# A DiT block kernel: the first residual's gate is summed in the merge loop instead of in the linear-attention heads

## The chip, the cores and the metric

The kernel runs on one core of a Trainium2 chip. The metric is the device time of one execution in microseconds; the lower the better. TensorE does the matmuls, VectorE, ScalarE and GpSimd the elementwise work, and SyncE issues the large DMAs.

## What is computed

One layer of a diffusion backbone on 512 latent tokens of width 1024, with 256 context tokens. A conditioning vector `c` gives, through one large matrix, six rows of 1024: shift, scale and gate of the token half, and shift, scale and gate of the channel half.

```python
mod = jax.nn.silu(c) @ w_ada[layer] + b_ada[layer]
sh1, sc1, gt1, sh2, sc2, gt2 = jnp.split(mod[:, None, :], 6, axis=-1)
h = modulate(rms_norm(x_lat, norm1_g[layer]), sh1, sc1)
mix, mix_c = token_mixer(h, hc, ...)      # MLA branch, GLA branch, sigmoid-gated merge, @ w_out
x_lat = x_lat + gt1 * mix
h = modulate(rms_norm(x_lat, norm2_g[layer]), sh2, sc2)
x_lat = x_lat + gt2 * conv_ffn(h, ...)
return rms_norm(x_lat, final_g)
```

`gt1` is the gate of the first residual. It is needed only when the merged branches have been multiplied by `w_out`. `sh2` and `sc2` are needed a little later, when the normalised rows are modulated for the channel half.

## The kernel before

Almost every matmul is done three times (`mm3`, L125 to L128) on operands split into a high and a low part. A split (`split`, L119 to L122) is a ScalarE cast for the high part and a subtraction, on GpSimd for most weights, for the low one. So a weight tile goes from a raw tile (three in turn, tag `raw`), filled by a DMA of the SyncE queue, through ScalarE and GpSimd into `whi` and `wlo` (four in turn each), and only then to TensorE.

The stages follow one another: the projections, eight heads of attention, the values of the linear attention (`gla_v`), four linear-attention heads, the merge loop over eight column blocks j of 128, `w_out` with the first residual and the second norm, the up projection with the convolution, and the down projection.

The modulation rows of the second half are made in parts of 256 columns by `mod_part` (L217). A part loads two tiles of 512 KB of `w_ada` and runs eight VectorE instructions over 128x256 elements (L227 once, L229 seven times), which leave in `mp` a sum over eight blocks of rows; the 128 partitions are still to be summed. `mod_fin` (L242) does that for shift and scale parts by two small matmuls with a column of ones (`mod_small`, L232) and a VectorE addition into `modsh2` or `modsc2`. `mod_bcast` (L255) does it for a gate part by a matmul of `ones` broadcast to 128x128 with the 256 columns, and adds the result into the gate's tile. Twelve parts are made ahead of `w_out`: eight of shift and scale (0 to 7) and four of the gate `gt1`.

In the kernel before, parts 0 and 1 are summed during the last attention heads and parts 2 and 3 during `gla_v`. Every linear-attention head h sums gate part h and, in its second half, part 4 + h; the last of each kind falls into the merge loop.

A linear-attention head does, on TensorE and in this order: transposes of the decayed keys (`to_tokens`, L875: those of the context from `C1` at L881, those of the latent tokens from `T1` at L885), the chunk states (`states`, L890) and the products within a chunk (`output`, L909). Before the states can start, VectorE has to copy the context transposes out of PSUM into `C2` (L882), and ScalarE those of the latent tokens into `T1` (L886, L887). The same VectorE also does the keys' and queries' scaling of the head (`apply`, L853), four passes over 128x1024 elements. In PSUM there are four single-bank tiles (`pb`) and two of two banks (`p2`, shown as `p` in the views).

The instruction order on each engine is set by a scheduler that simulates the program (`schedule_with_timeline_sim`), within the data dependences and the order in which tiles are handed out; the engines then run these lists strictly in order.

Of the kernel before, what the change touches and what calls it, by code (L numbers as in the profile page):

```python
# [9 lines left out]
F32 = mybir.dt.float32  # L10
# [62 lines left out]
def block_kernel(ctx: ExitStack, tc: tile.TileContext, p, out):  # L73
# [51 lines left out]
    def mm3(o, sh, sl, mh, ml, first, last):  # L125
        PE.matmul(o, lhsT=sh, rhs=mh, start=first, stop=False)  # L126
        PE.matmul(o, lhsT=sh, rhs=ml, start=False, stop=False)  # L127
        PE.matmul(o, lhsT=sl, rhs=mh, start=False, stop=last)  # L128

# [50 lines left out]
    def view(name):  # L180
# [4 lines left out]
                                         view("w_down"))  # L185

    def load_cols(w, c0, n=128, k0=0, k1=KT):
        r = raw_tile()
        SY.dma_start(out=k3(r, k1 - k0, n), in_=w[:, k0:k1, c0:c0 + n])
        return r  # L190
# [60 lines left out]

    def mod_norm2(j, tile_):
        return mod_part(3072 + j * 256, mp_tile(), tile_)

    def mod_bcast(acc, dst):  # L255

        ps = pb()
        mm(ps[:, 0:256], ones.broadcast_to([128, 128]), acc)
        tt(V, dst, dst, ps[:, 0:256], ALU.add)


# [28 lines left out]
    with tc.tile_pool(name="e1", bufs=1) as e1:  # L290
# [462 lines left out]
        for h in range(NH):  # L753
            P = softmax(h, q2s[h])
            if h == 0:
                for t in range(2, 6):
                    values(t)
                q2s.append(prep_q(1))
            if h + 1 < NH:
                prep_k(h + 1)  # L760
            if h + 2 < NH:
                q2s.append(prep_q(h + 2))
            if h == 5:
                gla_v_weights(0)
            attend(h, P)
            if h == 6:
                parts = [mod_norm2(0, S4f)]
            elif h == 7:
                parts.append(mod_norm2(1, S4f))
        heads_out(*pend[0])  # L770
        gla_v_weights(1)
        for t in range(6):
            gla_v(1, t)
            if t in (1, 3):
                mod_fin(t // 2, parts[t // 2])
                parts.append(mod_norm2(t // 2 + 2, S4f))

    def sigmoid(dst, ps):
        A.activation(dst, ps, AF.Exp, scale=-1.0)
        A.activation(dst, dst, AF.Ln, bias=1.0)  # L780
        A.activation(dst, dst, AF.Exp, scale=-1.0)

# [6 lines left out]
    with tc.tile_pool(name="egl", bufs=1) as eg:  # L789
# [192 lines left out]
        gr = gate(0)  # L982
        mod_fin(2, parts[2])
        mod_fin(3, parts[3])
        to_tokens(dec)
        for h in range(GH):
            St = states(h, dec)
            on = output(h, dec, Q, St)
            part = mod_part(2048 + h * 256, mp_tile(), S4f)
            if h + 1 < GH:  # L990
                dec = decay(h + 1)
                merge_mla(2 * h)
                kq = proj_kq(h + 1)
            else:
                merge_mla(2 * h)
                merge_mla(2 * h + 1)
            gate_out(h, on, gr)
            if h + 1 < GH:
                Q = apply(kq, dec)
                gr = gate(h + 1)  # L1000
                to_tokens(dec)
                mod_bcast(part, gt1[:, h * 256:(h + 1) * 256])
                part = mod_norm2(4 + h, S4f)
                merge_mla(2 * h + 1)
                mod_fin(4 + h, part)

# [7 lines left out]

    def load_wo(k):
        r = raw_tile()
        SY.dma_start(out=r, in_=w_out[:, k, :])
        h_, l_ = S4([128, 1024]), S4([128, 1024])
        split(h_, l_, r, V if k in (5, 7) else G)
        wo.append((h_, l_))  # L1020
# [11 lines left out]
    with tc.tile_pool(name="emg", bufs=1) as em_:  # L1032
        def merge_weights(j):
            return (split_w(load_cols(w_in, CGB + j * 128)), split_w(load_cols(w_brg, j * 128, k1=4), 512))

        ahead = merge_weights(0)
        for j in range(8):
            wgb, wbg = ahead
            gb = pb()
            proj(wgb, gb)  # L1040
            if j + 1 < 8:
                ahead = merge_weights(j + 1)
            bg = pb()
            for k in range(4):
                mm3(bg, k3(wbg[0], 4, 128)[:, k, :], k3(wbg[1], 4, 128)[:, k, :], yT[k][:, 0, :], yT[k][:, 1, :], k == 0,
                    k == 3)
            sg = tl(em_, [128, 512], F32, "sg", 2)
            sigmoid(sg, gb)
            tt(V, sg, bg, sg, ALU.mult)
            tt(V, sg, sg, m1[j // 2][:, j % 2, :], ALU.add)  # L1050
            mg[j] = S4([128, 2, 512])
            split(mg[j][:, 0, :], mg[j][:, 1, :], sg, V)
            if j in (1, 2, 3, 5):
                load_wo(len(wo))
            if j == 0:
                mod_bcast(part, gt1[:, 768:1024])
                part = mod_norm2(7, lambda: tl(em_, [128, 1024], F32, "xn", 2))
            elif j == 2:
                mod_fin(7, part)
        for k in range(4, 8):  # L1060
# [3 lines left out]
        def w_out_norm(t):  # L1064
            cs = slice(t * 128, (t + 1) * 128)
            mp = p2()
            for k in range(8):
                for half in range(2):
                    hs = slice(half * 512, (half + 1) * 512)
                    mm3(mp[:, hs], mg[k][:, 0, cs], mg[k][:, 1, cs], wo[k][0][:, hs], wo[k][1][:, hs], k == 0, k == 7)  # L1070
            xn = tl(em_, [128, 1024], F32, "xn", 2)
            for half in range(2):
# [202 lines left out]
```

## Time and profile before

| what | us |
|---|---|
| three runs: median | 931.99 |
| lowest and highest | 930.17, 933.8 |
| the profiled execution: its own time | 931.91 |
| its span, first to last instruction | 930.1 |
| TensorE busy in the span | 893.0 |

The profiled execution's time is 1.8 us more than its span, which is what lies around the program, and stands at the median of the runs. Times in the views count from the span's start. The linear-attention heads run from about 236 to 442 us, the merge loop from about 443 to 509 us.

### The profile page before, as it was taken

Reading aid. Unit: us, or ns where it says so; the run is one execution under the profiler, and the core shown is the slowest. Engines: PE = TensorE matmul, PEld = TensorE weight load, DVE = VectorE, ACT = ScalarE, POOL = GpSimd, SP = SyncE. Lnnn points to the kernel's source line nnn. Section 1 sums busy time; section 2 is a strip of 40 time slices with the busy share of each in tenths; the row PEclk is TensorE's granted clock in tenths of the full one; section 3 lists DMA queues with packets and bytes.
Section 4 is the critical chain, followed back from the end, with each engine's and each line's share of the span. In section 5 each row is a group of like instructions: output and inputs, shape, how many; then the busy total and the mean of one; then the engine's idle time right before and its main releaser. Section 6 shows DMA issues by size and latency. Waiting matters only on the chain. (4 is left out here: it accounts for less than half of the span.)

```text
span 930.1 us, 13004 instructions
## 1 busy us (share of the span) xinstructions
PE 893.0 (96%) x5012; PEld 760.0 (82%) x5012; DVE 599.8 (64%) x986; ACT 395.1 (42%) x653; POOL 383.7 (41%) x226
## 2 busy tenths in 40 slices
PE   4989999999989999999999999999999999999995
PEld 3768788899978888888888889888888888888884
DVE  3569987867886998984534484988687876300007
ACT  3445566764534545452445332443424333323102
POOL 3355133563232425242464621344445344466415
PEclk9999999999999999999999999999999999999998
DMA  9863000043341525152644521534343432244002
GB/s 302 258 168 103 1 1 1 9 129 110 107 125 35 161 66 162 55 158 69 212 139 125 164 63 47 157 92 146 103 137 90 136 109 96 73 158 154 23 1 90
DMA packets 131230, 100.77 MB, mean 108 GB/s; under 512 B 5755, under 2 KB 122723, under 8 KB 131169
## 3 DMA queue, kind: packets, MB, share of 16 engines
q1 hardware_dynamic: 130240, 97.83, 34.9%
q0 software_dynamic: 816, 2.09, 0.7%
q8 instruction: 39, 0.64, 0.3%
q14 instruction: 23, 0.18, 0.1%
q10 hardware_dynamic: 112, 0.04, 0.0%
HBM read 97.65 MB, written 2.10 MB: 107 GB/s over the span
## 5 line engine op out<-in xcount | busy, mean ns | idle before, releaser
L118 POOL TENSOR_TENSOR wlo<-raw,whi 128x1024 fp32r<-128x1024 f32 (+2 forms) x113 | 259.0, 2299 | 325.8 <-ACT whi L122 302.6
L126 PE MATMUL pb<-s,whi 128*128 128x512 f32 (+1 forms) x625 | 242.7, 388 | 0.1
L128 PE MATMUL pb<-s,wlo 128*128 128x512 f32 (+1 forms) x625 | 240.5, 385 | 0.0
L127 PE MATMUL pb<-s,whi 128*128 128x512 f32 (+1 forms) x625 | 240.2, 384 | 0.0
L122 ACT CAST whi<-raw 128x1024 fp32r<-128x1024 f32 (+1 forms) x108 | 106.2, 985 | 177.6 <-issue 76.6
L128 PEld LDWEIGHTS pb<-s,wlo 128*128 128x128 f32 x625 | 117.6, 188 | 23.1
L127 PEld LDWEIGHTS pb<-s,whi 128*128 128x128 f32 x625 | 117.7, 188 | 22.9 <-issue 0.7
L126 PEld LDWEIGHTS pb<-s,whi 128*128 128x128 f32 x625 | 117.7, 188 | 22.8 <-DVE modsc L115 0.3
L1146 DVE SCALAR_TENSOR_TENSOR ac<-pb,cwT,ac 128x441 f32<-128x441 f32 (+2 forms) x160 | 110.9, 693 | 19.1 <-ACT ac L1137 15.2
L115 DVE TENSOR_TENSOR ot<-p,gt 128x512 f32<-128x512 f32 x4 | 2.6, 686 | 98.2 <-PE p L128 98.2
L126 PE MATMUL pb<-whi,s 128*128 128x256 f32 (+1 forms) x168 | 55.2, 330 | 0.0
L229 DVE SCALAR_TENSOR_TENSOR mp<-s,csilu,mp 128x256 f32<-128x256 f32 x77 | 54.2, 715 | 1.5
L127 PE MATMUL pb<-wlo,s 128*128 128x256 f32 (+1 forms) x168 | 55.1, 328 | 0.0
L128 PE MATMUL pb<-whi,s 128*128 128x256 f32 (+1 forms) x168 | 55.0, 328 | 0.0
L126 PE MATMUL p<-s,s 128*128 128x512 f32 (+1 forms) x130 | 48.0, 370 | 5.3 <-DVE s L404 3.6
L686 POOL TENSOR_SCALAR P<-P,rs 128x768 f32<-128x768 f32 x32 | 29.4, 924 | 52.0 <-DVE rs L685 51.0
L127 PE MATMUL p<-s,s 128*128 128x512 f32 (+1 forms) x130 | 47.3, 365 | 0.3 <-DVE s L118 0.3
L128 PE MATMUL p<-s,s 128*128 128x512 f32 (+1 forms) x130 | 47.2, 363 | 0.0
L118 POOL TENSOR_TENSOR s<-raw,s 128x1024 fp32r<-128x1024 f32 (+1 forms) x14 | 33.3, 2389 | 26.7 <-ACT s L122 26.7
L128 PE MATMUL p<-s,wlo 128*128 128x256 f32 (+1 forms) x130 | 43.1, 331 | 0.0
L126 PE MATMUL p<-s,whi 128*128 128x256 f32 (+1 forms) x130 | 43.0, 331 | 0.0
L127 PE MATMUL p<-s,whi 128*128 128x256 f32 (+1 forms) x130 | 42.8, 329 | 0.0
(278 smaller groups left out, 1736.2 us busy)
## 6 DMA issues: line engine op xcount, KB each, us to landing
raw<-in_w_up_dram SPq DMA_DIRECT2D x44, 512.0 KB, 3.8
raw<-in_w_in_dram SPq DMA_DIRECT2D x32, 512.0 KB, 3.8
s<-in_w_ada_dram SPq DMA_DIRECT2D x30, 512.0 KB, 6.3
raw<-in_w_down_dram SPq DMA_DIRECT2D x22, 512.0 KB, 3.3
raw<-in_w_ada_dram SPq DMA_DIRECT2D x16, 512.0 KB, 4.8
raw<-in_w_out_dram SPq DMA_DIRECT2D x8, 512.0 KB, 3.4
kT<-in_w_in_dram SPq DMA_DIRECT2D x8, 320.0 KB, 5.3
s<-in_x_dram SPq DMA_DIRECT2D x4, 512.0 KB, 6.3
```

Source lines behind the costliest of these rows:

```text
L115: return eng.tensor_tensor(out=out_, in0=a, in1=b, op=op)
L118: eng.tensor_tensor(out=out_, in0=a, in1=b, op=ALU.subtract)
L122: A.copy(hi, src)
L126: PE.matmul(o, lhsT=sh, rhs=mh, start=first, stop=False)
L127: PE.matmul(o, lhsT=sh, rhs=ml, start=False, stop=False)
L128: PE.matmul(o, lhsT=sl, rhs=mh, start=False, stop=last)
L229: V.scalar_tensor_tensor(out=acc, in0=r3[:, k, :], scalar=c_, in1=acc, op0=ALU.mult, op1=ALU.add)
L686: G.tensor_scalar(out=pt, in0=pt, scalar1=rs, scalar2=1.0, op0=ALU.mult, op1=ALU.mult)
L1146: V.scalar_tensor_tensor(out=a3[:, r0:r1, c0:c1], in0=g3[:, r0 + dy:r1 + dy, c0 + dx:c1 + dx], scalar=cw(dy, dx), in1=a3[:, r0:r1, c0:c1], ...
```

## The change

The gate parts leave the heads. In the merge loop, blocks j = 0 to 3 each sum one gate part, straight into a quarter of one two-bank PSUM tile (`gsum`), from `w_ada` tiles of the pool `xn`, which gets three buffers instead of two; block 4 sums part 7 of the scale, in PSUM too. In block 6 ScalarE copies both sums to SBUF, and after block 7's matmuls two matmuls of 512 columns take the place of the four of 256 columns (`mod_bcast`), with two additions into `gt1`. The first four `w_out` tiles also load into `xn` instead of `raw`.

Parts 3 to 6 of the second norm are now begun in heads 0 to 3, one each, and the two small matmuls that end a part come one head later, behind `merge_mla` of the next head; those of parts 2 and 3 thus no longer stand ahead of the first head.

```diff
@@ attention heads and gla_v
-            if h == 6:
-                parts = [mod_norm2(0, S4f)]
-            elif h == 7:
-                parts.append(mod_norm2(1, S4f))
+            if h >= 6:
+                mod_begin(S4f)
...
             if t in (1, 3):
-                mod_fin(t // 2, parts[t // 2])
-                parts.append(mod_norm2(t // 2 + 2, S4f))
+                mod_end()
+            if t == 1:
+                mod_begin(S4f)
@@ linear-attention heads
         gr = gate(0)
-        mod_fin(2, parts[2])
-        mod_fin(3, parts[3])
         to_tokens(dec)
         for h in range(GH):
             St = states(h, dec)
             on = output(h, dec, Q, St)
-            part = mod_part(2048 + h * 256, mp_tile(), S4f)
             if h + 1 < GH:
                 dec = decay(h + 1)
                 merge_mla(2 * h)
+                mod_end()
                 kq = proj_kq(h + 1)
             else:
                 merge_mla(2 * h)
+                mod_end()
+                mod_begin(S4f)
                 merge_mla(2 * h + 1)
             gate_out(h, on, gr)
             if h + 1 < GH:
                 Q = apply(kq, dec)
                 gr = gate(h + 1)
                 to_tokens(dec)
-                mod_bcast(part, gt1[:, h * 256:(h + 1) * 256])
-                part = mod_norm2(4 + h, S4f)
+                mod_begin(S4f)
                 merge_mla(2 * h + 1)
-                mod_fin(4 + h, part)
@@ merge loop
+        def mraw():
+            return tl(em_, [128, 1024], F32, "xn", 3)
...
+        gsum = p2()
...
             if j in (1, 2, 3, 5):
-                load_wo(len(wo))
+                load_wo(len(wo), mraw)
             if j == 0:
-                mod_bcast(part, gt1[:, 768:1024])
-                part = mod_norm2(7, lambda: tl(em_, [128, 1024], F32, "xn", 2))
-            elif j == 2:
-                mod_fin(7, part)
+                mod_end()
+            with tc.issue_after(load[0].ins):
+                if j < 4:
+                    mod_part(2048 + j * 256, gsum[:, j * 256:j * 256 + 256], mraw)
+                elif j == 4:
+                    mod_begin(mraw, p2()[:, 0:256])
+            if j == 6:
+                m_, gm = mp_tile(), mraw()
+                with tc.issue_after(si.ins):
+                    A.copy(m_, begun[7])
+                    A.copy(gm, gsum)
+            elif j == 7:
+                with tc.issue_after(bg_.ins):
+                    mod_fin(7, m_)
+                    gp = p2()
+                    for half in range(2):
+                        hs = slice(half * 512, (half + 1) * 512)
+                        mm(gp[:, hs], ones.broadcast_to([128, 128]), gm[:, hs])
+                        tt(V, gt1[:, hs], gt1[:, hs], gp[:, hs], ALU.add)
```

`mod_begin` and `mod_end` are new and only keep count: the one calls `mod_part` for the next part, the other `mod_fin` for the oldest part begun. `issue_after` puts the block's instructions behind the named one in their engine's list.

The first place is VectorE at the start of the first linear-attention head, from the last two passes of `apply` to the gate's multiplication; `C` is C2, `T` is T1 or T2, `s` the scaled queries, `mp` a part's sum. Before:

```order
L115 TENSOR_TENSOR T_593_2838<-T_594_2839,ml_2864 128x1024
L115 TENSOR_TENSOR s_609_2969<-s_608_2968,ml_2864 128x1024
L115 TENSOR_TENSOR modsh_6_77<-pb_3011,pcol_72 128x2
L227 TENSOR_SCALAR mp_3106<-s_630_3107,csilu_76 128x256
L115 TENSOR_TENSOR modsh_6_77<-pb_3015,pcol_72 128x2
L229 SCALAR_TENSOR_TENSOR mp_3106<-s_630_3107,csilu_76,mp_3106 128x256
L882 COPY C_596_2841<-pb_3020 128x512
```

And after the change (line numbers are nine higher there):

```order
L115 TENSOR_TENSOR T_590_2825<-T_591_2826,ml_2851 128x1024
L115 TENSOR_TENSOR s_606_2956<-s_605_2955,ml_2851 128x1024
L891 COPY C_593_2828<-pb_2999 128x512
L115 TENSOR_TENSOR gr_2993<-pb_2968,gr_2993 128x512
L913 SCALAR_TENSOR_TENSOR S_3014<-S_3014,ml_2851,p_614_3013 128x128 x6
```

The copy of the context transposes now follows `apply` directly; four instructions ahead of it, and the gate part's others behind it, are gone.

The second place is TensorE there, from the end of the first head's gate projection to the first state. Before:

```order
L128 MATMUL pb_2981<-s_13_84,wlo_2978 128x512
L131 MATMUL pb_3011<-ones_74,mp_2693 128x1 x2
L131 MATMUL pb_3015<-ones_74,mp_2762 128x1 x2
L881 MATMUL pb_3020<-cst_71,C_595_2840 128x128 x4
L885 MATMUL p_617_3019<-cst_71,T_593_2838 128x128 x6
L131 MATMUL p_619_3034<-s_553_2515,C_596_2841 128x128 x2
```

And after:

```order
L128 MATMUL pb_2968<-s_13_84,wlo_2965 128x512
L890 MATMUL pb_2999<-cst_71,C_592_2827 128x128 x4
L894 MATMUL p_612_2998<-cst_71,T_590_2825 128x128 x6
L131 MATMUL p_614_3013<-s_553_2515,C_593_2828 128x128 x2
```

The two parts' small matmuls are gone from here; they come behind `merge_mla` of heads 0 and 1.

The third place is the SyncE queue early in the merge loop, from the reload of the tokens `x` on. Before:

```order
L1011 DMA x_854_4497<-in_x_dram 128x1024
L223 DMA xn_4580<-in_w_ada_dram 128x4x256
L223 DMA xn_4586<-in_w_ada_dram 128x4x256
L189 DMA raw_4682<-in_w_in_dram 128x8x128
L189 DMA raw_4688<-in_w_br_gla_dram 128x4x128
L1017 DMA raw_4716<-in_w_out_dram 128x1024
L189 DMA raw_4752<-in_w_in_dram 128x8x128
L189 DMA raw_4758<-in_w_br_gla_dram 128x4x128
L1017 DMA raw_4786<-in_w_out_dram 128x1024
```

And after:

```order
L1018 DMA x_838_4431<-in_x_dram 128x1024
L225 DMA xn_4516<-in_w_ada_dram 128x4x256
L225 DMA xn_4522<-in_w_ada_dram 128x4x256
L1024 DMA xn_4587<-in_w_out_dram 128x1024
L191 DMA raw_4636<-in_w_br_gla_dram 128x4x128
L191 DMA raw_4707<-in_w_in_dram 128x8x128
L225 DMA xn_4593<-in_w_ada_dram 128x4x256
L225 DMA xn_4599<-in_w_ada_dram 128x4x256
L191 DMA raw_4713<-in_w_br_gla_dram 128x4x128
L191 DMA raw_4784<-in_w_in_dram 128x8x128
L1024 DMA xn_4664<-in_w_out_dram 128x1024
```

Two `w_ada` tiles now stand between the weights of one block and those of the next, for blocks 0 to 4, and the `raw` tiles carry only the merge weights.

## Rows read from the trace of the kernel before

**Rows 1.** The page's first part: busy us, share of the span, instructions.

```profile
PE 893.0 (96%) x5012; PEld 760.0 (82%) x5012; DVE 599.8 (64%) x986; ACT 395.1 (42%) x653; POOL 383.7 (41%) x226
```

**Rows 2.** TensorE's waits, whole span: releaser, then us in total, times, longest.

```profile
PE p L131 <- DVE C L882: 3.0, 1, 3.0
PE p L126 <- ACT s L122: 1.7, 1, 1.7
```

**Rows 3.** TensorE's timeline, first head: start, duration, work, [idle before <- releaser].

```profile
267.71 0.95 PE L131 MATMUL pb<-ones,mp 128*128 128x1 f32 x8
268.52 0.64 PE L881 MATMUL pb<-cst,C 128*128 128x128 f32 x4
...
272.78 1.22 PE L131 MATMUL p<-s,C 128*128 128x128 f32 x4 [2.97 <-DVE C L882]
...
279.39 0.49 PE L131 MATMUL pb<-S,s 128*128 128x128 f32 x2
```

**Rows 4.** VectorE's timeline, first head, same columns.

```profile
268.03 1.22 DVE L115 TENSOR_TENSOR s<-s,ml 128x1024 f32<-128x1024 f32 x1
...
269.24 2.37 DVE L227 TENSOR_SCALAR mp<-s,csilu 128x256 f32<-128x256 f32 x1
...
272.05 0.68 DVE L882 COPY C<-pb 128x512 f32<-128x512 f32 x1
...
291.75 0.75 DVE L831 TENSOR_SCALAR T<-p,pcol 128x512 f32<-128x512 f32 x1 [1.17 <-ACT T L830]
```

**Rows 5.** GpSimd's timeline, first head.

```profile
268.86 2.60 POOL L118 TENSOR_TENSOR wlo<-raw,whi 128x1024 fp32r<-128x1024 f32 x1 [3.09 <-ACT whi L122]
290.77 2.41 POOL L118 TENSOR_TENSOR wlo<-raw,whi 128x1024 fp32r<-128x1024 f32 x1 [19.31 <-ACT whi L122]
```

**Rows 6.** ScalarE's timeline, first head.

```profile
270.23 0.48 ACT L887 COPY T<-p 128x384 f32<-128x384 f32 x1
```

**Rows 7.** Stretches: from:to, length, busy of five engines, PEclk, DMA share, GB/s.

```profile
272.00:274.00 2.00, 1.22 (x5) 1.22 (x6) 1.93 (x5) 0.00 (x0) 0.00 (x0) 0.58 0.44 131
...
276.00:278.00 2.00, 2.00 (x27) 1.73 (x26) 0.83 (x3) 0.43 (x2) 0.00 (x0) 1.00 0.00 0
```

**Rows 8.** TensorE's timeline, second head, and one row of the third.

```profile
321.61 0.60 PE L131 MATMUL p<-s,C 128*128 128x128 f32 x4
...
327.17 0.49 PE L131 MATMUL pb<-S,s 128*128 128x128 f32 x2
...
328.26 0.38 PE L131 MATMUL pb<-s,s 64*128 64x256 f32 x1 [0.29 <-DVE s L115]
...
376.14 0.38 PE L131 MATMUL pb<-s,s 64*128 64x256 f32 x1 [0.35 <-DVE s L115]
```

**Rows 9.** VectorE's timeline, second head.

```profile
319.10 8.50 DVE L229 SCALAR_TENSOR_TENSOR mp<-s,csilu,mp 128x256 f32<-128x256 f32 x10
327.52 0.68 DVE L115 TENSOR_TENSOR s<-pb,sg 128x512 f32<-128x512 f32 x1
```

**Rows 10.** Instructions that write `mp`: duration in ns, smallest/median/largest, first and last start.

```profile
L229 DVE SCALAR_TENSOR_TENSOR mp<-s,csilu,mp x77: 459/484/2709, 217.9 to 421.0; 128x256 f32<-128x256 f32 x77
```

**Rows 11.** Stretches, columns as in rows 7: the start, the projections, the merge loop.

```profile
0.00:40.00 40.00, 26.80 (x261) 20.97 (x261) 14.96 (x45) 14.59 (x30) 14.91 (x25) 1.00 0.98 310
40.00:80.00 40.00, 36.73 (x280) 29.48 (x280) 30.39 (x57) 21.68 (x42) 23.32 (x22) 1.00 0.52 146
...
442.00:484.00 42.00, 42.00 (x191) 34.82 (x190) 18.21 (x25) 18.89 (x29) 22.38 (x12) 1.00 0.56 176
```

**Rows 12.** TensorE's timeline: first matmul of merge block 5, first of `w_out`.

```profile
484.45 0.39 PE L126 MATMUL pb<-s,whi 128*128 128x512 f32 x1
...
508.93 0.39 PE L126 MATMUL p<-s,s 128*128 128x512 f32 x1
```

**Rows 13.** ScalarE's and GpSimd's timelines: the split of block 5's weights.

```profile
479.48 1.05 ACT L122 CAST whi<-raw 128x1024 fp32r<-128x1024 f32 x1 [3.70 <-DMA raw<-in_w_in_dram]
480.61 4.11 POOL L118 TENSOR_TENSOR wlo<-raw,whi 128x1024 fp32r<-128x1024 f32 x2 [2.85 <-ACT whi L122]
```

More of the change, by code (lines that the diff above doesn't have):

```diff
@@ L127, in mm3 @@
         PE.matmul(o, lhsT=sh, rhs=ml, start=False, stop=False)
-        PE.matmul(o, lhsT=sl, rhs=mh, start=False, stop=last)
+        return PE.matmul(o, lhsT=sl, rhs=mh, start=False, stop=last)
     def mm(o, a, b, first=True, last=True):
@@ L185, in block_kernel @@
                                          view("w_down"))
+    load = [None]
     def load_cols(w, c0, n=128, k0=0, k1=KT):
         r = raw_tile()
-        SY.dma_start(out=k3(r, k1 - k0, n), in_=w[:, k0:k1, c0:c0 + n])
+        load[0] = SY.dma_start(out=k3(r, k1 - k0, n), in_=w[:, k0:k1, c0:c0 + n])
         return r
@@ L250, in mp_tile @@
         return sm(256, "mp", 2)
-    def mod_norm2(j, tile_):
-        return mod_part(3072 + j * 256, mp_tile(), tile_)
     def mod_bcast(acc, dst):
@@ L259, in mod_bcast, with mod_begin, mod_end @@
         tt(V, dst, dst, ps[:, 0:256], ALU.add)
+    begun, ended = [], [0]
+    def mod_begin(tile_, acc=None):
+        begun.append(mod_part(3072 + len(begun) * 256, mp_tile() if acc is None else acc, tile_))
+    def mod_end():
+        j = ended[0]
+        ended[0] += 1
+        mod_fin(j, begun[j])
     hTh = [S4([128, 2, 512]) for _ in range(4)]
@@ L780, in sigmoid @@
         A.activation(dst, dst, AF.Ln, bias=1.0)
-        A.activation(dst, dst, AF.Exp, scale=-1.0)
+        return A.activation(dst, dst, AF.Exp, scale=-1.0)
     yT = [None] * GH
@@ L1013, in block_kernel, with load_wo @@
     wo = []
-    def load_wo(k):
-        r = raw_tile()
+    def load_wo(k, tile_=raw_tile):
+        r = tile_()
         SY.dma_start(out=r, in_=w_out[:, k, :])
@@ L1044, in block_kernel @@
             for k in range(4):
-                mm3(bg, k3(wbg[0], 4, 128)[:, k, :], k3(wbg[1], 4, 128)[:, k, :], yT[k][:, 0, :], yT[k][:, 1, :], k == 0,
+                bg_ = mm3(bg, k3(wbg[0], 4, 128)[:, k, :], k3(wbg[1], 4, 128)[:, k, :], yT[k][:, 0, :], yT[k][:, 1, :], k == 0,
                     k == 3)
             sg = tl(em_, [128, 512], F32, "sg", 2)
-            sigmoid(sg, gb)
+            si = sigmoid(sg, gb)
             tt(V, sg, bg, sg, ALU.mult)
@@ L1070, in w_out_norm @@
                     mm3(mp[:, hs], mg[k][:, 0, cs], mg[k][:, 1, cs], wo[k][0][:, hs], wo[k][1][:, hs], k == 0, k == 7)
-            xn = tl(em_, [128, 1024], F32, "xn", 2)
+            xn = mraw()
             for half in range(2):
```

## The prediction

> **What bounds the kernel now.** The page's first part comes first: TensorE is busy for 893.0 of the 930.1 us of the span [rows 1]. A change to the other engines can therefore gain only what TensorE waits, and what it loses by a lowered clock. So the next view is TensorE's waits. Most of them lie in the start and in the attention part, which the change doesn't touch. In the linear-attention heads, the merge loop and `w_out`, one stands out: 3.0 us, once, for VectorE's copy `C2` at L882 [rows 2]. TensorE's timeline puts it in the first head: the small matmuls of parts 2 and 3 at 267.71, ten transposes from 268.52, then 2.97 us of nothing, and the first state at 272.78 [rows 3]. VectorE's timeline tells why the copy was late. The last pass of `apply` begins at 268.03 and lasts 1.22 us; then comes the gate part's first instruction, which takes 2.37 us, and only at 272.05 the copy, 0.68 us long [rows 4]. The slow one lies under a GpSimd subtraction from 268.86 to 271.46 [rows 5].
>
> The stretches show a second price of this stop. From 272 to 274 us the granted clock is 0.58, which means the lower level, 1.2 GHz, for most of the stretch; from 276 us it is 1.00, 2.4 GHz [rows 7]. The states of the first head thus ran slowly: from their first matmul to the first one of the output there are 6.61 us (272.78 to 279.39) [rows 3], against 5.56 us in the second head (321.61 to 327.17) [rows 8], where four rows of small matmuls lie between as well. By eight such rows in 0.81 us (267.71 to 268.52) [rows 3] these are 0.40 us, so the same states take 5.16 us at full clock, and the low clock cost 1.45 us.
>
> Two more stops of this kind are 0.29 us in the second head and 0.35 us in the third; both wait for VectorE at L115 [rows 8]. VectorE comes to that multiplication, `s<-pb,sg` at 327.52, behind a run of ten part instructions that starts at 319.10 [rows 9].
>
> **The change part by part.** The sum is made against the profiled execution, 931.91 us, which stands at the median of the runs, 931.99.
>
> *The first head.* The copy now follows `apply` directly. TensorE's and VectorE's lists are the same up to there, apart from part instructions on VectorE that go, so the last pass of `apply` still ends at about 269.2 (268.03 plus 1.22) [rows 4] and the copy at 269.9. TensorE doesn't run the eight small rows first, so its transposes end 0.81 us sooner, at 269.0 instead of 269.8 (272.78 less 2.97 is 269.81) [rows 3]. It waits 0.9 us, not 2.97, and starts the states at 269.9 instead of 272.8: 2.9 us sooner. The eight rows are not saved but run in the next two heads, 0.8 us, so 2.1 us remain. ScalarE's second copy of the transposes, which the later states need, ended at 270.71 [rows 6], and is not later now: at worst some 0.3 us of waiting inside the states. The other end is a copy that comes earlier still and leaves no wait: 3.0 us.
>
> *The clock there.* With a stop of 0.9 us I expect the clock to stay up, a gain of 1.45 us. The nearest row is a stop of 1.7 us for ScalarE [rows 2], in the stretch from 40 to 80 us with a mean granted clock of 1.00 [rows 11]. The bounds are 0 and 1.45. The Trainium skill, TensorE: Matmul & The Clock Gate, section "Part 1: The HAM clock gate", says that the low clock is the default and that activity releases it. By that sentence a short stop among light work could still cost the clock, and the sum would be 929.2; the trace speaks against it with the stop of 1.7 us.
>
> *The second and third head.* With one part per head instead of two, eight instructions fewer stand ahead of the multiplication. A part's instruction has a median of 0.484 us [rows 10]; eight are 3.9 us, against 0.29 and 0.35 us of waiting. Both stops go: 0.6 us.
>
> *The merge loop, VectorE.* There 32 part instructions more run. The trace has none that sums in PSUM. The bounds are 0.46 us, the smallest of those in SBUF [rows 10], and 0.85 us, the mean of the run of ten in 8.50 us, which shared the stretch with GpSimd [rows 9]: 15 to 27 us. I take the median, 0.484 us [rows 10], 15.5 us together. VectorE is idle for 23.8 of the 42 us from 442 to 484 us [rows 11], and the loop goes on to 508.93 [rows 12], so even the upper bound is caught up by its end. No matmul of the loop needs a part; what could wait behind them is `sg`, whose products TensorE needs only at `w_out`. Cost: nothing; without that cover, if VectorE got no further than its idle time up to 484 us, `w_out` could wait 3 us.
>
> *The merge loop, transfers.* Four parts of two 512-KB tiles come in, 4.2 MB. The block's weights must land, be cast and subtracted in time. Before, block 5's cast began at 479.48, right when its DMA had landed, and the low part was ready at about 483 [rows 13]; TensorE began the block at 484.45 and needs the low part with its third matmul [rows 12], so there are about 2 us in hand. After the change those `raw` tiles no longer alternate with `w_out` tiles, so a block's weights can be asked for a tile earlier, but in the SyncE queue two `w_ada` tiles stand ahead of them, and these wait for a buffer in `xn`. A block takes 8.16 us of TensorE (484.45 to 508.93 is three of them) [rows 12]. The stretch moves 176 GB/s now [rows 11]; 4.2 MB more over 42 us add 100, which gives 276. In the first 40 us the chip moved 310 at a DMA share of 0.98 [rows 11]. It fits, with a tenth to spare: cost nothing, and see the rivals.
>
> *The rest.* Two matmuls of 512 columns for four of 256 are the same columns; ScalarE's two copies lie in a loop where it is busy 18.9 of 42 us [rows 11]; the wait for them is over before block 7 ends. Nothing.
>
> The sum: 2.1 + 1.45 + 0.6 = 4.2 us, so 927.7 us, a change of 0.45%.
>
> **The rivals.**
>
> *The clock falls all the same.* The gain is then 2.7 us: 929.2. For it: ten light transposes and a stop still stand before the states. Against it: the 1.7 us stop. Chance 0.16.
>
> *The copy is held up in its new place.* It would now run beside the GpSimd subtraction from 268.86 to 271.46 [rows 5], beside which a part instruction with its data in SBUF took 2.37 us [rows 4]. If the copy were held until 271.5, the states would begin at 272.2, 0.6 us sooner, of which the moved rows take 0.8; the clock falls, the small stops go, and the time is 931.5, no change. Against it: a VectorE instruction that reads PSUM ran 0.75 us at 291.75 [rows 4], in the middle of another such subtraction [rows 5]. The Trainium skill, VectorE: DVE Perf Modes, section "Two Vector instructions with no wait between them", speaks of a second SBUF read interface that VectorE shares with GpSimd; an instruction whose only tensor lies in PSUM would not use it, and the trace agrees (0.75 us). Chance 0.07.
>
> *The merge weights come late: slower.* Blocks 1 to 3 move weights, a `w_out` tile and a gate part, 0.79 + 0.52 + 1.05 = 2.36 MB in 8.16 us, 289 GB/s. If the queue, which stops whenever an `xn` tile isn't free, gave only today's 176 GB/s, a block would take 13.4 us, and blocks 1 to 3 alone would be 15.7 us late: 943. At 256 GB/s a block loses 1.06 us, blocks 0 to 3 together 4.2, and the gain is gone; below about 230 the kernel is slower by over 0.5%. For it: the cast that waited for its DMA [rows 13]. Against it: 310 GB/s at the start, and weights that are now loaded a tile ahead. The Trainium skill, DMA: Bandwidth & Descriptors, section "Measured (HBM→SBUF, 128 partitions, SWDGE, issued from GpSimd)", asks for transfers of at least 1 MiB, and these are half of that; the trace's start is made of transfers that small and smaller, and reached 310. Chance 0.10, half of it past the bound.
>
> *No wait is left at the copy.* 0.9 us more: 926.8. Chance 0.10; the other 0.57 are my forecast.
>
> **How the numbers follow.** 927.7 is the likeliest case. A measurement can tell about 0.5% from no change, 4.7 us here, and the forecast lies just inside it. The runs shown differ by up to 1.8 us from their median, so the forecast and its better variant come out past 927.3 in about half of their 0.67; with the rest I put 0.36 on faster, 0.57 on the same and 0.07 on slower. The range for 8 in 10 goes from 925.3, the best case less some scatter, to 931.2, which takes in the lowered clock, and a little of the held copy and of late weights.
>
> **What the profile will show.** If I am right: in the first head the copy directly behind `apply`, under 1 us of idle ahead of the first state, a granted clock of 1.00 in the two microseconds behind it, no idle at L115 in the second and third head, and no wait of TensorE in the merge loop or `w_out`. Wrong would be: a clock near 0.6 behind the first states, the copy at 0.7 us turned into 2 or more, or TensorE waiting for `whi` or `wlo` in the merge loop, with the queue standing at an `xn` tile.

## The result and the profile after

| | before | changed |
|---|---|---|
| median of 10 runs each, same chip, us | 933.52 | 926.34 |
| lowest and highest, us | 930.17, 938.38 | 923.91, 930.99 |
| ratio, 95% interval | | 0.9928 [0.9902, 0.9953] |

The change makes the kernel faster: 0.72% is 6.7 us, and the interval reaches from 4.4 to 9.1 us. (The two medians by themselves differ by 7.2.) The forecast was a gain of 4.2 us, just inside the 0.5% that it took a measurement to be able to tell. The interval here ends a little inside that mark, at 0.47%; that of a second set of runs (0.59 to 0.86%, below) lies beyond it.

The page's first part, to be held against [rows 1]: TensorE's busy time hardly moves. So the gain lies in when TensorE waits and how fast it is clocked.

```profile
PE 894.5 (96%) x5008; PEld 760.4 (82%) x5008; DVE 588.5 (63%) x984; ACT 396.6 (43%) x655; POOL 384.2 (41%) x226
```

TensorE's waits (us in total, times, longest). The wait for `C2`, 3.0 us in [rows 2], is 1.0; no row of L115 is left, and none of a split weight (`whi`, `wlo`). The second row lies in the start, at 53 us.

```profile
PE p L131 <- DVE C L891: 1.0, 1, 1.0
...
PE p L126 <- ACT s L122: 2.1, 1, 2.1
```

TensorE's timeline (start, duration, work, [idle before <- releaser]). The first four rows answer to [rows 3]; the others are the first row of the states of heads 1 and 3, the place of the former L115 stop in head 1 with the matmul behind it ([rows 8]), and the first row of the up projection.

```profile
270.50 0.60 PE L890 MATMUL pb<-cst,C 128*128 128x128 f32 x4
270.95 0.87 PE L894 MATMUL p<-cst,T 128*128 128x128 f32 x6
272.78 0.68 PE L131 MATMUL p<-s,C 128*128 128x128 f32 x4 [0.95 <-DVE C L891]
...
277.97 0.49 PE L131 MATMUL pb<-S,s 128*128 128x128 f32 x2
...
319.61 0.60 PE L131 MATMUL p<-s,C 128*128 128x128 f32 x4
...
325.14 0.38 PE L131 MATMUL pb<-s,s 64*128 64x256 f32 x2
325.45 0.50 PE L126 MATMUL pb<-s,whi 128*128 128x512 f32 x1
...
413.18 0.60 PE L131 MATMUL p<-s,C 128*128 128x128 f32 x4
...
620.68 0.59 PE L131 MATMUL pb<-mp,ones 128*128 128x256 f32 x2
```

VectorE's timeline ([rows 4]): the copy now stands directly behind the last pass of `apply`.

```profile
270.82 1.22 DVE L115 TENSOR_TENSOR s<-s,ml 128x1024 f32<-128x1024 f32 x1
271.95 0.68 DVE L891 COPY C<-pb 128x512 f32<-128x512 f32 x1
```

GpSimd's timeline ([rows 5]): its subtraction lies over the copy in its new place.

```profile
271.64 2.61 POOL L118 TENSOR_TENSOR wlo<-raw,whi 128x1024 fp32r<-128x1024 f32 x1 [3.08 <-ACT whi L122]
```

Stretches (from:to, length, busy time of PE, PEld, DVE, ACT, POOL, then PEclk, DMA share, GB/s). The granted clock is 1.00 where it was 0.58 [rows 7]; in the merge loop VectorE is busy 9.9 us longer than in [rows 11], and the transfers go at 293 instead of 176 GB/s, while TensorE is never idle.

```profile
272.00:274.00 2.00, 1.22 (x11) 1.25 (x12) 0.63 (x2) 1.97 (x5) 2.00 (x1) 1.00 0.00 1
276.00:278.00 2.00, 2.00 (x31) 1.59 (x30) 1.40 (x6) 0.00 (x0) 0.00 (x0) 1.00 0.26 77
442.00:484.00 42.00, 42.00 (x189) 34.84 (x188) 28.08 (x49) 22.59 (x33) 24.91 (x12) 1.00 0.90 293
```

Vector instructions on the gate tiles (`xn`) with their sum in PSUM (`p`): smallest, median and largest duration in ns.

```profile
L231 DVE SCALAR_TENSOR_TENSOR p<-xn,csilu,p x35: 476/490/491, 453.3 to 489.4; 128x256 f32<-128x256 f32 x35
L229 DVE TENSOR_SCALAR p<-xn,csilu x5: 486/487/489, 452.8 to 483.5; 128x256 f32<-128x256 f32 x5
```

**The time between landmarks.** The profiled spans (930.1 and 927.7 us) differ by only 2.4 us, because the start of the program, which the change leaves alone, took longer in the second. So the table counts from the end of the first head's gate projection (267.71 before [rows 3], 270.50 after), each entry being the difference of two starts on TensorE's timeline. Both kernels were profiled again, as runs of their own (below).

| us from ... to ... | before | before, again | before, third | after | after, again |
|---|---|---|---|---|---|
| gate projection's end, states of head 0 | 5.07 | 5.08 | 5.07 | 2.28 | 2.29 |
| states of head 0, of head 1 | 48.83 | 50.22 | 50.22 | 46.83 | 46.86 |
| states of head 1, of head 2 | 48.18 | 49.78 | 49.84 | 46.79 | 46.75 |
| states of head 2, of head 3 | 47.67 | 47.67 | 47.70 | 46.78 | 46.79 |
| states of head 3, up projection | 205.71 | 205.71 | 205.71 | 207.50 | 207.49 |
| up projection, end | 306.93 | 306.93 | 307.00 | 307.02 | 306.95 |
| sum | 662.4 | 665.4 | 665.5 | 657.2 | 657.1 |

From that point on the changed kernel takes the same time to 0.1 us, and the kernel before does not: the gain is 5.2 us against its first profile and 8.3 against the other two.

### The profile page after: what moved, and what is told of

Its sections match the earlier page's. It is cut to its first block, busy times and chain, and to the rows that moved or that the text cites. A ratio compares the mean times of both kernels' runs of the same rounds, so it can differ in the third digit from the quotient of the medians.

```text
span 927.7 us, 12994 instructions
## 1 busy us (share of the span) xinstructions
PE 894.5 (96%) x5008; PEld 760.4 (82%) x5008; DVE 588.5 (63%) x984; ACT 396.6 (43%) x655; POOL 384.2 (41%) x226
## 5 line engine op out<-in xcount | busy, mean ns | idle before, releaser
L115 DVE TENSOR_TENSOR ot<-p,gt 128x512 f32<-128x512 f32 x4 | 2.6, 686 | 98.2 <-PE p L128 98.2
L126 PE MATMUL p<-s,s 128*128 128x512 f32 (+1 forms) x130 | 48.6, 375 | 6.0 <-DVE s L414 3.9
L128 PE MATMUL p<-s,s 128*128 128x512 f32 (+1 forms) x130 | 48.1, 370 | 0.0
L127 PE MATMUL p<-s,s 128*128 128x512 f32 (+1 forms) x130 | 47.8, 368 | 0.3 <-DVE s L118 0.3
L1175 ACT ACTIVATE ac<-ac 128x512 f32<-128x512 f32 x22 | 13.9, 632 | 67.7 <-DVE ac L1173 67.7
L118 DVE TENSOR_TENSOR pl<-pb,ph 128x512 fp32r<-128x512 f32 x48 | 32.3, 683 | 12.2 <-ACT ph L727 12.0
```

Of the source, the lines that this page charges most:

```text
L115: return eng.tensor_tensor(out=out_, in0=a, in1=b, op=op)
L118: eng.tensor_tensor(out=out_, in0=a, in1=b, op=ALU.subtract)
L128: return PE.matmul(o, lhsT=sl, rhs=mh, start=False, stop=last)
L1175: gelu.append(A.activation(ac, ac, AF.Gelu))
```

## The experiments

**Both kernels once more.** No edit.

> The changed kernel, unchanged, for a second profile and more pairs of times. Theory 1 (the gain is that of the heads, 5.2 us from the end of the gate projection on, the rest of the first difference is scatter of the start): ratio near 0.9945, and 657.2 us from the end of the gate projection to the end, within 0.3. Theory 2 (the gain is really 6.7 us or more): ratio near 0.9928 again, and more than 5.2 us to be found between two profiles with the same start.

> The kernel before, unchanged, profiled a second time. Theory 1 (the stretch ahead of the linear-attention heads differs from execution to execution, the rest does not): from the end of the first head's gate projection to the end the span is again 662.4 us within 0.3, with the stop of about 3 us at the copy C2 and a clock near 0.6 behind it, while the end of the gate projection may lie up to 3 us away from 267.7. Theory 2 (the heads themselves scatter): the 662.4 us differ by 1 us or more.

> The kernel before once more, for a third profile of its first two heads. Theory one (the clock behind its stops varies from one execution to the next): from the end of the first gate projection to the end it takes 661 to 667 us, with a granted clock of 0.6 or less in one or two stretches behind the first stop and, in some executions, 0.75 to 0.85 behind the second head's. Rival (the second profile was an outlier for a reason outside these heads): 662 to 663 us, as in the first profile.

Measured: the changed kernel 925.73 us, ratio 0.9928 [0.9914, 0.9941]; the kernel before 935.43 and 933.15 us in the single runs that were profiled. What varies in the kernel before is the clock. Stretches of its third profile:

```profile
272.00:276.00 4.00, 4.00 (x23) 3.88 (x24) 1.78 (x4) 0.40 (x2) 0.00 (x0) 0.50 0.00 0
276.00:280.00 4.00, 4.00 (x44) 3.14 (x42) 2.73 (x9) 0.20 (x2) 0.00 (x0) 0.87 0.01 2
328.00:332.00 4.00, 4.00 (x11) 3.09 (x11) 3.92 (x12) 1.82 (x4) 0.00 (x0) 0.57 0.02 4
```

TensorE is fully busy in all three, and still at or near the lower level: 0.50 is 1.2 GHz. The third stretch lies behind the L115 stop of head 1, 0.29 us of idle here too. In the first profile that stop left the clock at 1.00 and the stage took 48.18 us, here 49.84. The expectation that the first profile was the rule falls; it was the mildest of three. Nor is the gain only the 5.2 us of the first two profiles: the ratio came out at 0.9928 again.

**The kernel before, only its order changed.** In the first of two kernels the copy of the first head goes ahead of the gate part's instructions, and the small matmuls of parts 2 and 3 go a head later; nothing moves to the merge loop:

```diff
-        mod_fin(2, parts[2])
-        mod_fin(3, parts[3])
-        to_tokens(dec)
+        cp = to_tokens(dec)
...
-            part = mod_part(2048 + h * 256, mp_tile(), S4f)
+            if h == 0:
+                with tc.issue_after(cp.ins):
+                    part = mod_part(2048, mp_tile(), S4f)
+            else:
+                part = mod_part(2048 + h * 256, mp_tile(), S4f)
```

> The kernel before, with only the first head mended: the sums of gate part 0 are put behind the copy C2 in VectorE's list, and the small matmuls of parts 2 and 3 come behind merge_mla of heads 0 and 1. No part leaves the heads. Theory 1 (the order of VectorE's list at the copy made the stop and with it the low clock): 3.5 us are gained (2.1 and 1.4), the stop there is 0.9 to 1.0 us and the clock 1.00 behind it; ratio 0.9962. The stops of 0.3 us in heads 1 and 2 may stay. Theory 2 (VectorE's load in the heads has to fall for it): VectorE is late at the copy or later in the head all the same, and less than 2 us are gained.

In the second, the gate and scale parts of all heads also go behind the last multiplication of `merge_mla(2 * h + 1)`, with their small matmuls a head later:

```diff
-                part = mod_norm2(4 + h, S4f)
-                merge_mla(2 * h + 1)
-                mod_fin(4 + h, part)
+                cp = merge_mla(2 * h + 1)
+                with tc.issue_after(cp.ins):
+                    late = mod_norm2(4 + h, S4f)
```

> As the run before it, and in the later heads the sums of gate and scale parts stand behind the multiplication s<-pb,sg of the same head, with their small matmuls a head later. All parts stay in the heads, the merge loop is that of the kernel before. Theory 1 (order alone): all three stops are gone or below 1 us, the gain is that of the change: 4.9 to 5.2 us from the end of the gate projection on, ratio 0.9945. Theory 2 (moving the load to the merge loop is worth something of its own): at least 1 us less gain than the change in the same runs.

Measured: 927.84 us, 0.9950 [0.9936, 0.9965], and 929.05 us, 0.9961 [0.9947, 0.9976]. By its ratio, either gets more than half of the gain without the merge loop, though both intervals reach to a little less than half. From the gate projection's end their profiles take 659.5 and 658.9 us, against 657.2 of the change. The first head takes 2.28 us to its states in both, exactly as in the change. What is missing is a stop further on. TensorE's waits of the first of the two kernels, then of the second:

```profile
PE pb L131 <- DVE s L115: 0.4, 1, 0.4
```

```profile
PE p L885 <- DVE T L115: 1.5, 1, 1.5
```

In the first the stop in head 2 stays, and in its profile the clock falls behind it (the stage takes 49.30 us instead of 46.78):

```profile
372.00:376.00 4.00, 3.65 (x9) 2.78 (x10) 3.88 (x14) 2.21 (x4) 0.00 (x0) 0.60 0.03 6
```

In the second the parts' instructions are late elsewhere: `apply` comes late, and the transposes of `T1` wait 1.5 us. With 16 part instructions in a head, moving them moved the stop in both orders tried; taking eight away removed it. That no order could do with all 16 is not shown.

**How long a stop may be.** The changed kernel, with the copy `C2` of the first head made three or five times in a row:

```diff
-            V.tensor_copy(C2, grp(tc_, 2))
+            for _ in range(times):
+                V.tensor_copy(C2, grp(tc_, 2))
```

> The changed kernel with the copy C2 of the first head done three times over (the same data), which puts the states off by twice 0.61 us. Theory 1 (a stop costs its own length, and clock only when it is near 3 us): the stop is 2.2 us instead of 0.95, the clock stays 1.00, 1.2 us slower from the gate projection on. Theory 2 (the clock falls for shorter stops too): the clock behind the stop is near 0.6 and 2.6 us are lost.

> The same with the copy done five times: the states are put off by four times 0.61 us, 2.4 us. Theory 1 and 2 both: the stop is 3.4 us, as long as that of the kernel before; the clock falls to near 0.6 for 3 to 4 us, which costs 1.4 us more, 3.8 us in all from the gate projection on. If the clock stays at 1.00 here, the low clock of the kernel before was not made by the length of the stop alone.

Measured: 928.44 us, 0.9957 [0.9936, 0.9978], and 932.07 us, 0.9993 [0.9976, 1.0010]. The wait of the first head and the stretch behind it, with three copies, then both with five:

```profile
PE p L131 <- DVE C L892: 2.4, 1, 2.4
```

```profile
276.00:280.00 4.00, 4.00 (x27) 3.20 (x26) 2.78 (x7) 2.10 (x4) 0.00 (x0) 1.00 0.00 0
```

```profile
PE p L131 <- DVE C L892: 4.3, 1, 4.3
```

```profile
276.00:280.00 4.00, 4.00 (x26) 3.93 (x26) 0.00 (x0) 0.23 (x2) 0.00 (x0) 0.57 0.00 0
```

From the gate projection's end the two take 658.7 and 662.1 us, 1.5 and 4.9 more than the change. The stop of 2.4 us costs its own length more (2.4 less 0.95 is 1.45); that of 4.3 costs about 3.35 by its length and 1.6 by the clock (from the states of head 0 to those of head 1, 48.47 us against 46.83 to 46.86). It is 4.3 and not the 3.4 expected, because a copy takes 0.7 us here and VectorE's list puts the gate's multiplication between the fourth copy and the fifth. So the time that the copy holds TensorE up and the clock behind it are two prices, as the forecast had it, here with one profile for each length. The 0.95 us of the change stand in eight profiles, and the clock is 1.00 behind all of them.

**Is it the PSUM sum, or when the sum is closed?** The first kernel sums in SBUF and closes each part one block later, as the heads did:

```diff
+            if 1 <= j <= 4:
+                mod_bcast(gpart, gt1[:, (j - 1) * 256:j * 256])
...
-                    mod_part(2048 + j * 256, gsum[:, j * 256:j * 256 + 256], mraw)
+                    gpart = mod_part(2048 + j * 256, mp_tile(), mraw)
```

> The changed kernel with the merge loop's sums in SBUF tiles (mp) instead of PSUM; each gate part is closed by its own matmul of 256 columns one block later, as in the kernel before, and the two copies of ScalarE are gone. Theory 1 (where the sums lie is hidden by TensorE's 100% in the loop): the same time as the changed kernel within 0.5 us in the profile from the gate projection on; the part instructions beside GpSimd's subtractions get longer than 0.5 us. Theory 2 (the sums in PSUM keep VectorE and GpSimd out of each other's way, and that is needed): TensorE waits for whi or wlo in the merge loop, 1 to 5 us.

It changes two things at once. A second one changes only the place of the sums, which makes ScalarE's two copies needless, and closes them behind block 7, as the change does:

```diff
-        gsum = p2()
+        gsum = S4f()
...
-                    mod_begin(mraw, p2()[:, 0:256])
+                    mod_begin(mraw)
-            if j == 6:
-                m_, gm = mp_tile(), mraw()
-                with tc.issue_after(si.ins):
-                    A.copy(m_, begun[7])
-                    A.copy(gm, gsum)
```

> The changed kernel with the gate parts of the merge loop summed in SBUF instead of PSUM, and closed after the last block as in the changed kernel, so without the two copies of ScalarE. It separates the two things that the kernel with the sums in SBUF closed one block later changed at once. Theory one (the closing matmul inside the loop made TensorE wait, not the sums' place): the stop of 5.2 us goes and the time is the changed kernel's, 926 to 927. Rival (the sums' place): VectorE's part instructions run at 2.4 us where GpSimd splits beside them, the block's own multiplications come late, TensorE waits in the loop or before the output projection, and the time is 929 to 935.

Measured: 935.26 us, 1.0024 [1.0008, 1.0041], and 930.35 us, 0.9990 [0.9976, 1.0003]. From the states of head 3 to the up projection they take 215.70 and 212.36 us, against 207.50: the place of the sums costs 4.9 us, the early closing 3.3 more. Theory one of the second run falls: the place is the larger part. A wait of TensorE and two stretches of the first kernel, where a closing matmul stands in TensorE's list while VectorE is still at that sum:

```profile
PE pb L131 <- DVE mp L231: 5.2, 1, 5.2
```

```profile
456.00:460.00 4.00, 0.14 (x1) 0.14 (x1) 3.82 (x7) 0.62 (x1) 1.26 (x1) 0.61 0.65 202
460.00:464.00 4.00, 4.00 (x10) 3.20 (x11) 3.22 (x8) 1.56 (x2) 0.18 (x1) 0.53 0.76 234
```

In the second kernel the wait is elsewhere, and it can be followed backwards over four engines at one of the three places. Its Vector instructions on `xn`, sums in SBUF (`s`):

```profile
L231 DVE SCALAR_TENSOR_TENSOR s<-xn,csilu,s x28: 475/485/2559, 449.9 to 489.1; 128x256 f32<-128x256 f32 x28
```

TensorE, GpSimd, ScalarE and VectorE there, each from its timeline:

```profile
487.41 0.50 PE L128 MATMUL pb<-s,wlo 128*128 128x512 f32 x1 [1.92 <-POOL wlo L118]
```

```profile
471.96 2.50 POOL L118 TENSOR_TENSOR s<-xn,s 128x1024 fp32r<-128x1024 f32 x1 [6.09 <-ACT s L122]
474.42 4.00 POOL L118 TENSOR_TENSOR wlo<-raw,whi 128x1024 fp32r<-128x1024 f32 x2
482.36 2.50 POOL L118 TENSOR_TENSOR s<-xn,s 128x1024 fp32r<-128x1024 f32 x1 [3.95 <-PE pb L128]
484.82 3.96 POOL L118 TENSOR_TENSOR wlo<-raw,whi 128x1024 fp32r<-128x1024 f32 x2
```

```profile
480.71 0.62 ACT L122 CAST s<-sg 128x512 fp32r<-128x512 f32 x1 [5.55 <-DVE sg L115]
481.24 1.04 ACT L122 CAST s<-xn 128x1024 fp32r<-128x1024 f32 x1
482.19 1.05 ACT L122 CAST whi<-raw 128x1024 fp32r<-128x1024 f32 x1
```

```profile
471.71 7.50 DVE L231 SCALAR_TENSOR_TENSOR s<-xn,csilu,s 128x256 f32<-128x256 f32 x5
479.13 0.68 DVE L115 TENSOR_TENSOR sg<-pb,sg 128x512 f32<-128x512 f32 x1
```

Five part instructions take 7.50 us, most of it under GpSimd's subtractions from 471.96 to 478.42. So VectorE finishes `sg` late; ScalarE, whose list has the cast of `sg` ahead of those of the weights, stands 5.55 us; GpSimd gets the `w_out` tile and then the block's weights late (its wait at 482.36 is put down to TensorE, but the cast that it needs ends only at 482.28); and TensorE waits 1.92 us for `wlo`. Nothing ties the weights to the sums but the order of two lists.

**The transfers.** In the change, with `w_out` tiles back in `raw` (`load_wo(len(wo))` in place of `load_wo(len(wo), mraw)`):

> The changed kernel with the w_out tiles of blocks 1, 2, 3 and 5 loaded into raw again. Theory 1 (the merge weights have enough in hand): no wait of TensorE in the merge loop, the same time within 0.5 us from the gate projection on. Theory 2 (with w_ada tiles in the queue, the weights need raw for themselves): the cast of a block's weights comes later than 5 us ahead of the block, and TensorE waits for whi or wlo, 1 to 6 us in all.

And the change with every `w_ada` tile of the loop's gate parts loaded twice into the same place, 4.2 MB more:

```diff
-            SY.dma_start(out=r3, in_=w_ada[:, k0:k0 + 4, c0:c0 + 256])
+            for _ in range(times):
+                SY.dma_start(out=r3, in_=w_ada[:, k0:k0 + 4, c0:c0 + 256])
```

> The changed kernel with each of the eight gate tiles of the merge loop loaded twice into the same place, 4.2 MB more in the loop (the second load is the same data). Theory one (the transfers have headroom there, the stretches move 201 and 227 GB/s now and the sums' ends are not urgent): the stretches show 250 to 280 GB/s, no new TensorE wait, 926 to 927.5. Rival (the transfers are near their limit in the loop): the merge weights land late, TensorE waits for the splits of the block's weights, 929 to 938, with a lowered clock behind the stops.

Measured: 929.97 us, 0.9968 [0.9955, 0.9981], and 929.50 us, 0.9974 [0.9955, 0.9994]. With the tiles in `raw` the stage takes 3.1 us more than the change's and TensorE waits for the block's weights:

```profile
PE pb L128 <- POOL wlo L118: 2.2, 2, 1.4
```

With doubled loads it takes 2.4 us more. The stretches show transfers at about 300 GB/s through the whole loop:

```profile
440.00:460.00 20.00, 20.00 (x92) 16.64 (x91) 8.02 (x13) 9.50 (x15) 9.26 (x5) 1.00 0.95 320
460.00:480.00 20.00, 20.00 (x90) 16.57 (x89) 12.67 (x22) 8.80 (x13) 10.17 (x6) 1.00 0.88 285
480.00:500.00 20.00, 20.00 (x90) 16.57 (x89) 13.23 (x25) 10.61 (x16) 10.15 (x5) 1.00 0.96 313
```

The weights are still in time. TensorE's wait is for a sum, ScalarE's copy at L1078, which on ScalarE's timeline stands behind the cast of a `w_out` tile that landed late:

```profile
PE pb L131 <- ACT mp L1078: 1.3, 1, 1.3
```

```profile
503.54 1.04 ACT L122 CAST s<-xn 128x1024 fp32r<-128x1024 f32 x1 [1.91 <-DMA xn<-in_w_out_dram]
504.49 0.36 ACT L1078 COPY mp<-p 128x256 f32<-128x256 f32 x1
```

Neither theory of that run had this wait. The change's own stretches show 308, 282 and 172 GB/s there, not the 201 and 227 that the expectation gives. The change has room for its own 4.2 MB and not for the same again.

**The last 0.95 us.** The change with the context transposes and `C2` ahead of the gate projection, by a `to_tokens_c` of their own that is called before `gate(h)`:

> The changed kernel with the four context transposes and the copy C2 put ahead of the gate projection in every head, so that VectorE makes the copy before the last passes of apply; nothing else is changed. Theory one (what is left of the first head's stop, 0.95 us, is the copy's place behind apply): the stop goes, or shrinks to the 0.2 to 0.6 us that ScalarE's copies of the transposes still cost, and the kernel is 0.3 to 0.9 us faster than the changed one, 925.5 to 926. Rival: in the later heads the context product on GpSimd comes late for transposes that stand earlier, TensorE waits there at the transposes, and the time is 927 to 929.

Measured: 926.04 us, 0.9944 [0.9923, 0.9966], which can't be told from the change's 0.9928. In its profile the copy is done early, at 260.51, and TensorE's wait is now 0.7 us for ScalarE's copy of `T1`. From the start of the first head's gate projection (here, of the transposes ahead of it) to the end it takes 662.2 us, in the change's two profiles 662.6: 0.4 us, at the lower end of what was expected, and too little for the runs to show.

## Why the prediction was right in kind and short in size

**The first head.** Right. The copy follows `apply` and TensorE waits 0.95 us (forecast 0.9). The states start 2.28 instead of 5.07 us behind the gate projection, 2.79 sooner (forecast 2.9), of which 0.81 are moved rows: 1.98 us of the stop itself.

**The held copy.** Did not happen: 0.68 us under GpSimd's subtraction.

**The clock.** Right for this stop: with 0.95 us the clock stays at 1.00, and the first head's states take 5.19 us (272.78 to 277.97) as forecast (5.16). They took 6.61 us in the first profile of the kernel before and 8.00 in the two others. So the term of 1.45 us measured 1.42 against the execution from which it was read and 2.81 against the others; its size was that of the mildest. The Trainium skill, TensorE: Matmul & The Clock Gate, section "Part 1: The HAM clock gate", says that the number of slow matmuls at a kernel's start differs from run to run of one kernel; the three profiles agree for the place behind this stop, where they differ by 1.4 us.

The row on which the forecast leaned does not carry it, and there it had luck. The wait for ScalarE in the start was 1.71 us in the first profile of the kernel before and 1.67 in the second. The stretch behind it, in the first and then in the second:

```profile
56.00:60.00 4.00, 4.00 (x47) 2.69 (x46) 1.62 (x3) 0.94 (x3) 1.54 (x2) 1.00 0.96 231
56.00:60.00 4.00, 4.00 (x31) 2.98 (x30) 1.59 (x2) 0.50 (x2) 1.09 (x2) 0.81 0.82 205
```

All fourteen profiles have this wait, with 1.53 to 2.08 us; the clock fell there in seven and stayed at 1.00 in seven. The stop of 1.7 us was thus no evidence that the clock stays up.

**The products of the first head.** The stage from head 0 to head 1 is 2.00 us shorter against the first profile and 3.39 against the others. A broadcast matmul (0.44 us) went from it and two small ones (0.45) came, which is nothing, and the clock is 1.42 or 2.81. Some 0.43 of the rest is a thing that the forecast did not have. Two 64x512 products of `output` stand apart in TensorE's list of the kernel before; in its third profile:

```profile
285.11 0.50 PE L131 MATMUL p<-s,s 64*128 64x512 f32 x1
...
287.97 0.49 PE L131 MATMUL p<-s,s 64*128 64x512 f32 x1
```

The next row starts 0.43 us behind either. In the changed kernel the two are one row, x2, at 282.78, and the next row starts at 283.21: side by side, the two take as long as one. They do so in the two kernels with only the order changed as well. Some 0.15 us of the stage stay unexplained.

**The second and third head.** This is the step that failed, by its size. I put the two L115 stops at their idle time, 0.6 us. The first of them, before, with [rows 8] between these two:

```profile
327.59 0.38 PE L131 MATMUL pb<-s,s 64*128 64x256 f32 x1
...
328.57 0.50 PE L126 MATMUL pb<-s,whi 128*128 128x512 f32 x1
```

Start to start, the two 64x256 products take 0.98 us before and 0.31 after (325.14 to 325.45 above), where they run side by side, so the stop costs 0.67 with 0.29 of idle shown. From head 1 to head 2 the stage is 1.39 us shorter; 0.72 of that are small rows that moved out, which leaves 0.67. From head 2 to head 3 it is 0.89 shorter, with small rows of the same length as before. That is 1.56 us in the profile on which the forecast rests. In the two others the clock falls behind the first of these stops too, and it is 3.2 (2.27 to 2.33, and 0.9). I had asked what a long stop does to the clock and not what a short one costs. The merge loop shows the same: with the sums in SBUF three waits, 3.9 us in all, go with 4.9 us more, and with `w_out` tiles in `raw` two waits, 2.2 us, with 3.1.

**The merge loop, VectorE.** Right: an instruction takes 0.49 us (forecast 0.484), and nothing waits. But the cover is the place of the sum. My upper bound for it, 0.85 us from SBUF sums, would not have been "caught up": at a mean of 1.1 us (31.0 us for 28) the run with SBUF sums lost 4.9 us. I looked for what needs a part; what got hurt was what stands behind it, `sg`, and behind that in ScalarE's list the weights. That sums in PSUM escape GpSimd is shown by 476 to 491 ns over all 35, against up to 2559 in SBUF. The Trainium skill, VectorE: DVE Perf Modes, section "Two Vector instructions with no wait between them", lets an instruction with two SBUF tensor inputs read the second through the interface that GpSimd shares; with its sum in PSUM a part instruction has only one, and these numbers agree.

**The merge loop, transfers.** Right: forecast 276 GB/s, measured 293, no wait. It depends on `w_out` tiles being in `xn`.

**The rest.** Nearly right. Two matmuls of 512 columns took 1.80 us where four of 256, at 0.44, are 1.76; from head 3 on the kernel is 1.88 us longer, against 1.51 (0.81 and 0.72, less 0.01 in each of two stages) of rows that left the stages ahead: 0.37 lost.

The sum against the first profile: 1.98 + 2.00 + 1.56, less 0.37, is 5.2. Against the other two profiles the gain is 8.3. The measured 6.7 lies between. So the forecast was short by 1 us in the profile that it read, for the stops at L115 and the pair of products, and by 3 us more against the other executions, in which the clock fell further and in one place more.

## What to carry to other kernels

A short stop of TensorE costs more than its idle time, and two products of 64 rows that run side by side cost what one costs: keep such a pair together in TensorE's list, look at starts on both sides of a stop, and profile the kernel before more than once, because the clock behind the same stop can differ. Where VectorE accumulates beside GpSimd, put the sum in PSUM, and close it with a matmul that stands where the sum is long done. A part of VectorE's list that nobody waits for still delays what stands behind it, and a cast in the next engine's list carries that to the weights.

## What the runs showed of the hardware

The clock behind a stop did not follow the stop's length alone: stops of 0.95 us (eight profiles) and 2.4 (one) left it at 1.00, those of 2.97 (three) and 4.3 (one) brought it to 0.5 to 0.6, those of 1.53 to 2.08 in the start did either, and one of 0.29 us left it up in one execution of the kernel before and brought it down in two, to 0.57 over 4 us in the third profile.

The start of the program, the same instructions in every kernel here, scatters: the first head's gate projection ended between 265.3 and 270.5 us. Part of it is the clock. It fell behind the wait for ScalarE at 53 us in seven of the fourteen profiles, and between 84 and 92 us in seven. Where it fell at neither place the projection ended between 265.3 and 267.7 us, at one of them between 266.8 and 268.4, at both between 269.7 and 270.5 (leaving out the run that has transposes ahead of it). A stretch of the changed kernel, where it fell at both, and the same of the run with `w_out` tiles in `raw`, whose profile has the earliest end:

```profile
80.00:120.00 40.00, 36.65 (x187) 31.18 (x186) 32.92 (x67) 18.98 (x38) 5.39 (x5) 0.91 0.10 27
80.00:120.00 40.00, 36.57 (x209) 30.90 (x208) 34.40 (x73) 21.64 (x43) 5.71 (x6) 1.00 0.05 13
```

Why the clock fell there in one and not in the other stays open; no run was made on the start.
